# Attention in a hybrid layer on Trainium2: adding DMAs issued apart from their plain loads, and scans a half step later

## The chip, the core and the metric

One core of a Trainium2 chip runs the whole program. The metric is the device time of one execution in microseconds (us), the median over executions. A core has TensorE (PE, matrix products; its weight loads are listed as PEld), VectorE (DVE), ScalarE (ACT), GpSimd (POOL) and SyncE (SP). Each works through its own list of instructions in order and stops at an instruction whose inputs are not there.

## What is computed

One inference step of one decoder layer, for 16 meta tokens, a prompt of 512 tokens and 8 running sequences of 4 new tokens each (560 tokens), width 1024, all in float32:

```python
h = x + 0.5 * rms_norm(swiglu(rms_norm(x, ffn1_pre_g), ffn1_w_gate, ffn1_w_up, ffn1_w_down), ffn1_post_g)
u = rms_norm(h, mix_pre_g)
proj = u @ w_in            # q_a, k_a, v_a, gk_low, r_a of the GLA branch; q_b, k_b, v_b; gate_a, gate_b
...
z = jnp.einsum('bqhd,bkhd->bhqk', qblk, k).astype(jnp.float32) * scale + bias_f
mask = k_idx[None, :] < qi[:, None]
l = jnp.where(mask, jax.nn.log_sigmoid(-z), 0.0)
r = lax.cumsum(l, axis=3, reverse=True) - l
a = jnp.where(mask, jnp.exp(jax.nn.log_sigmoid(z) + r), 0.0)
return jnp.einsum('bhqk,bkhd->bqhd', a.astype(v.dtype), v)
...
m = jax.nn.sigmoid(gate_a) * (o_a @ w_o_gla) + jax.nn.sigmoid(gate_b) * (o_b @ w_o_sb)
h = h + rms_norm(m @ w_out, mix_post_g)
y = h + 0.5 * rms_norm(swiglu(rms_norm(h, ffn2_pre_g), ffn2_w_gate, ffn2_w_up, ffn2_w_down), ffn2_post_g)
```

The change concerns the stick-breaking attention (the middle block): 16 heads of 64, with strictly causal weights. A weight A[t,s] is the sigmoid of its score times the product of (1 - sigmoid) over the later positions before t. The sampled tokens attend to a paged cache as well, in other instructions of the same stages.

## The kernel before

**Stages.** In order of time: FFN1 (to about 400 us), the GLA branch (to about 590), the attention (about 590 to 820), the output products of the mixer, and FFN2. In the attention stage the projections q_b, k_b, v_b are computed for one pair of heads after the other, 8 pairs. Tokens lie on the free axis of a tile, 560 columns in two halves of 280. A float32 product is made of three products of parts in the matmul's own format: hi by hi, hi by lo, lo by hi. So every weight tile that comes from DRAM (a "raw") is first split: ACT casts it to its hi part, and DVE subtracts that from the raw for its lo part (`tt`, L172).

**Order.** The order on PE, DVE, ACT and POOL is the order in which the code emits instructions; only SP's queue, which issues the plain loads, is left to a scheduler. The code counts half steps: one `yield` of a product loop is a half step, some 6 matmuls of 280 columns. `then(n, f)` runs `f` behind half step `n`, `later(d, f)` runs it `d` half steps on. Pair `pr` begins at half step `BEGIN[pr]` = 0, 24, 46, 68, 90, 112, 134, 156. From pair 1 on, its **main** part has 8 half steps of `queries` (`tile_steps`, L723 to L726) and 14 of `values_keys` (`seven_steps`, L1074 hi by hi, L1075 hi by lo, L1076 lo by hi). "Main 3" below is the main part of pair 3, and "+14" is the half step 14 behind its begin.

**The weights of keys and values.** `seven_steps` computes the two products with seven block products in place of eight: it uses b1 twice, t, b2, t, b2, t4, where t and t4 are sums of weight blocks. `weights_at` sets when each of the four is split: hi by `parts_of` (ACT, L1001) and lo by `parted_lo` (DVE, L172). Counted from the pair's begin, b1 has hi at +2 and lo at +3, t has +5 and +6, b2 has +10 and +11, t4 has +13 and +15. PE first uses b2 after +14. Its product goes on into the accumulator d, so the copy e5 of d (ACT, L1054) must have been made by then.

**Adding DMAs.** Two of the sums, t1 and t3, are partly made by the DMA. `Chunks.fetch` takes the next chunk of weights. If it is of kind "adding", it starts plain loads on SP's queue (L644, L645, L652), and issues on POOL's queue a DMA that adds a second operand in place (L648 into the raw, L653 into the room of t3). The adding DMA waits for the plain loads, and it is an instruction in POOL's list. `fetch` runs in main `pr` at +3 (first chunk of pair pr+1), +11 (second chunk) and +18 (the queries' weights of pair pr+2, plain). There are seven DMAs of each of L648 and L653.

**The attention of a pair.** While PE computes main `pr`, the attention of pair `pr`-1 goes on between its half steps, for head 0 and head 1 of the pair (called (0,n) and (1,n), n the part of the score matrix):

- `scores` at +2, +3, +5, +7, +10, +12: PE's products, ACT's two sigmoids (L2002 and L2003: `keep` and `beta`), POOL's masks on `beta` (`affine_select`, L2007).
- `scan` at +3, +3, +5, +6 for head 0 and +8, +9, +11, +13 for head 1: DVE's running product along `keep` (L2016).
- `weigh` at +9 and +14: DVE multiplies `beta` and `keep` (L172, 128x1343), and makes two small copies (L2027). It needs the masks and the scans of its head.
- `turned`, from +15 on: PE transposes the weights (L2078), ACT and DVE make hi and lo of them. The first three calls are for head 0 and the next three for head 1.
- `rows_v` and `rows_k` at +6 and +11 and `tails` at +12: transposes for the new cache rows.

Once, in main 2, `sample_rows` puts a memset and four selects on POOL (L2142 to L2148) at +8, and `sample_rows_out` transposes that on PE (L2160) at +13.

**The end of queries.** The projected queries are scaled and split too: four casts on ACT (L1920) and, for the lo parts, four `stt` on DVE (L175). Behind them four small operations on DVE (L1929) put the sampled tokens' queries into the tiles `qz`.

**Rooms.** Large tiles are taken from and given back to an arena of SBUF; the table `PLACES` says which place each `take` gets. Where a new tile lies on the place of an old one, its writer waits for the old one's readers.

Of the kernel before, what the change touches and what calls it, by code (L numbers as in the profile page):

```python
# [14 lines left out]
ALU = mybir.AluOpType  # L15
# [38 lines left out]
1824062b1f3c5a12107a7792469472788c90324c6a888286487e8e3a68804a0284406c7c643655448a30622f1666607050524e0c3874426e560c  # L54
5e5404340002765957121e5a2e202c2a0c14224a163a68566c7c80643e3c8a3036628444501a4e746e703866422428266001060a3448946a8646
8e924c905a5488325f1a188276727e0d5600025057738c094e5b5d78043e548272075e1c7e0c3c0b835051187f5a8c5976583e1a5306565e5f73
0a4e550c7e8382725a508c3d5276545e065c0b0c58573c83085a733d7e764172555e8c0c5257828d060a583c085476837240590c7e8c578d0655
580c52543c3d823e7606728c598d7e57540f0c0e823c0d76528c7e72949084648e20147c7086600668380e6a086c6224223642803a2c66922e2a
821a4c181c0c4e6a50065a2e540a57092c822a3c6a0b084e2d2f2c820b062b2a4f834e2a2e830b824e2a2c2d2b5a0c422a2e3f3c0b3e82781a83
88386a41541c4a8e6448183c4c7e6c6290348c123050544e32860a6026282441562092701e1563191d4d798f229466842c3e2a2e004b7f89656d  # L60
1b8a49083b096858367459396e72040073027c56403c578a8014686a1658156072569226572825241470719228201e9484223e2c66242e562a14
865c5e628c70063444468e5a4210676c82641876787e88520b4c1c4a3b0f0e482c081a380a66142e257026641258188c305c6c820c9467849224
4a4c767e5e2a627822481c633b3e86205054291e700a66144a082e27644c1a1684948e0e255a5e1f0692672a427e3812783b626386341e227032
76255446524e502324293e6c4482922e7e275658662a42784a18144b708c7a1011060a385e5c3b1c20889008861213302e22921e94846662327e
5a8234425876648e787a388c7027480c5630122a1c1a920d4d11173421821e207e273256182a921248821e5b0c17342c2e7e494d5a2027305692
4821327e34102a82125b561e48190c0e215b181720329227344d827e1c1a102a56481230341e5a2c2e18124d175f327e9256271c1a8216304918
# [70 lines left out]
def hybrid_step(  # L137
# [36 lines left out]
    def stt(out, a, s, b, op0, op1):  # L174
        V.scalar_tensor_tensor(out=out, in0=a, scalar=s, in1=b, op0=op0, op1=op1)  # L175
# [454 lines left out]
    class Chunks:  # L630


        def __init__(self, todo):
            self.todo, self.raws, self.parts, self.early, self.rooms = list(todo), [], [], {}, []
# [2154 lines left out]
```

## Time and profile before

| | |
|---|---|
| executions timed | 1514.03 us median of 3 (1513.37 to 1514.87) |
| the profiled execution | 1517.31 us, of it 1515.6 us span |
| granted TensorE clock, mean | 0.991 |
| PE busy | 1488.7 us, 98% of the span |
| DVE, ACT, POOL busy | 1100.7 (73%), 821.0 (54%), 89.3 (6%) us |
| attention stage, 590 to 820 us | PE busy 211.87 of 230 us |
| adding DMAs, issue to landing, median | 5.2 us (L648), 6.2 us (L653) |

The profile's rows give times in us from the start of the span. In a timeline row stand the start, the duration, the engine, the line and the operation, output and inputs, shapes and, in brackets, how long the engine had been idle before it and what released it. Where rows of one kind follow each other they are one row with a count (x4) and the time from the first one's start to the last one's end. In a table of windows stand, for PE, PEld, DVE, ACT and POOL, the busy time and number of instructions of each, then the granted clock of TensorE (1.00 is full speed), the busy share of the DMA engines and GB/s.

### The profile page before, as it was taken

The page shows a single profiled execution, that of the slowest core. Times are in us where ns is not written, and L with a number is a line of the kernel's source. Part 1 is how long each engine was busy: PE and PEld are TensorE (multiplying, and loading weights), DVE is VectorE, ACT ScalarE, POOL GpSimd, SP SyncE. Part 2 cuts the span into 40 slices and gives each one's busy share as a digit, 9 for nine tenths or more (in the row PEclk, how much of TensorE's full clock was granted, in tenths as well). Part 3 has the DMA queues.
Part 4 walks back from the last instruction along what each step waited for, and adds up shares of the span by engine and source line. Part 5 has one row for each costly group of instructions (what it writes and reads, how often), then busy time and mean ns, then how long its engine had stood idle before and what let it go on. Part 6 is the DMA issues. An engine that isn't in the chain of part 4 may idle for free.

```text
span 1515.6 us, 29815 instructions
## 1 busy us (share of the span) xinstructions
PE 1488.7 (98%) x11825; PEld 1436.4 (95%) x11825; DVE 1100.7 (73%) x1860; ACT 821.0 (54%) x1537; POOL 89.3 (6%) x175
## 2 busy tenths in 40 slices
PE   9999999999999999899999999999999999999998
PEld 8999999999999888788889999999999999999998
DVE  5888888945677767677778745666567998888544
ACT  6445444533655647566777644644565554455434
POOL 2000000000000021321212000000000000000000
PEclk9999999999999999899999999999999999999999
DMA  8133333234664694447566776435532233333343
GB/s 248 54 88 99 98 98 99 86 100 143 165 140 138 161 184 112 100 91 127 122 120 164 213 182 209 101 96 138 158 101 87 87 101 100 108 98 86 89 143 121
DMA packets 288541, 187.61 MB, mean 124 GB/s; under 512 B 10988, under 2 KB 266674, under 8 KB 288402
## 3 DMA queue, kind: packets, MB, share of 16 engines
q1 hardware_dynamic: 280706, 181.97, 45.0%
q0 software_dynamic: 7680, 3.74, 2.4%
q8 instruction: 93, 1.52, 0.4%
q14 instruction: 46, 0.38, 0.1%
q10 hardware_dynamic: 16, 0.00, 0.0%
HBM read 160.63 MB, written 25.03 MB: 123 GB/s over the span
## 4 chain that ended last, share of the span: by engine, by line
PE 91%; DVE 4%; DMA 1%; ACT 1%; issue 1%; POOL 1%; SPq 1%; DVEq 0%; POOLq 0%; ACTq 0%
PE acc L1295 8%; PE acc L1297 8%; PE acc L1296 7%; PE acc L736 6%; PE acc L737 6%; PE acc L739 6%; PE acc L723 5%; PE acc L724 4%; PE acc L726 4%; PE acc L1074 4%; PE acc L1076 4%; PE acc L1075 4%; PE acc L1237 2%; PE acc L1234 2%; PE acc L1235 2%; DVE room L172 1%
## 5 line engine op out<-in xcount | busy, mean ns | idle before, releaser
L172 DVE TENSOR_TENSOR room<-room,room 128x544 f32<-128x544 f32 (+16 forms) x439 | 285.6, 669 | 98.5 <-ACT room L803 18.0
L172 DVE TENSOR_TENSOR lo<-raw,hi 128x1024 fp32r<-128x1024 f32 (+1 forms) x207 | 248.3, 1200 | 82.4 <-ACT hi L701 44.3
L1297 PE MATMUL acc<-room,lo 128*128 128x280 f32 (+1 forms) x896 | 259.6, 290 | 0.0
L1295 PE MATMUL acc<-room,hi 128*128 128x280 f32 (+1 forms) x896 | 259.5, 290 | 0.0
L1296 PE MATMUL acc<-room,hi 128*128 128x280 f32 (+1 forms) x896 | 259.2, 289 | 0.0
L1001 ACT CAST hi<-raw 128x1024 fp32r<-128x1024 f32 x114 | 119.5, 1052 | 141.7 <-PE acc L1296 49.1
L723 PE MATMUL acc<-room,hi 128*128 128x280 f32 x608 | 175.7, 306 | 0.2 <-DVE room L175 0.2
L1295 PEld LDWEIGHTS acc<-room,hi 128*128 128x128 f32 x896 | 168.8, 188 | 0.0
L1296 PEld LDWEIGHTS acc<-room,hi 128*128 128x128 f32 x896 | 168.8, 188 | 0.0
L1297 PEld LDWEIGHTS acc<-room,lo 128*128 128x128 f32 x896 | 168.5, 188 | 0.0
L724 PE MATMUL acc<-room,hi 128*128 128x280 f32 x608 | 163.8, 288 | 0.0
L1074 PE MATMUL acc<-room,hi 128*128 128x280 f32 x476 | 150.1, 315 | 2.2 <-ACT room L1054 1.9
L1076 PE MATMUL acc<-room,lo 128*128 128x280 f32 (+1 forms) x476 | 141.8, 298 | 7.4 <-DVE lo L172 7.4
L1075 PE MATMUL acc<-room,hi 128*128 128x280 f32 (+1 forms) x476 | 140.7, 296 | 0.0
L701 ACT CAST hi<-raw 128x1024 fp32r<-128x1024 f32 (+1 forms) x93 | 93.6, 1006 | 75.8 <-issue 20.4
L1001 ACT CAST hi<-room 128x1024 fp32r<-128x1024 f32 x106 | 88.6, 836 | 81.8 <-PE acc L1296 60.7
L172 DVE TENSOR_TENSOR lo<-room,hi 128x1024 fp32r<-128x1024 f32 x106 | 100.9, 952 | 43.3 <-ACT hi L1001 43.1
L726 PE MATMUL acc<-room,lo 128*128 128x280 f32 x608 | 125.9, 288 | 0.0
L723 PEld LDWEIGHTS acc<-room,hi 128*128 128x128 f32 x608 | 114.5, 188 | 7.3 <-issue 5.6
L724 PEld LDWEIGHTS acc<-room,hi 128*128 128x128 f32 x608 | 114.6, 189 | 0.6
L736 PE MATMUL acc<-room,hi 128*128 128x280 f32 (+2 forms) x388 | 110.7, 295 | 0.0
L737 PE MATMUL acc<-room,hi 128*128 128x280 f32 (+2 forms) x388 | 108.8, 290 | 0.0
(408 smaller groups left out, 3644.1 us busy)
## 6 DMA issues: line engine op xcount, KB each, us to landing
raw<-in_w_in_dram SPq DMA_DIRECT2D x68, 256.0 KB, 4.9
raw<-in_ffn_w_gate_dram SPq DMA_DIRECT2D x64, 256.0 KB, 3.1
raw<-in_ffn_w_up_dram SPq DMA_DIRECT2D x64, 256.0 KB, 3.4
raw<-in_ffn_w_down_dram SPq DMA_DIRECT2D x36, 448.0 KB, 3.8
raw<-in_w_in_dram SPq DMA_DIRECT2D x29, 512.0 KB, 7.9
out_dram<-room SPq DMA_DIRECT2D x36, 256.0 KB, 3.7
room<-in_cache_k_dram SPq DMA_DIRECT2D x32, 256.0 KB, 5.9
room<-in_cache_v_dram SPq DMA_DIRECT2D x32, 256.0 KB, 4.7
```

The costliest lines, as they stand in the source:

```text
L172: (eng or V).tensor_tensor(out=out, in0=a, in1=b, op=op)
L723: T.matmul(acc[h][:, :w], hi[k], act.get(k, h, w)[0], start=(k == order[0]), stop=False, skip_group_check=True)
L724: T.matmul(acc[h][:, : wid[h]], hi[k], a[h][1], start=False, stop=False, skip_group_check=True)
L736: T.matmul(acc[h][:nw, : wid[h]], wh, a[h][0], start=(k == 0), stop=False)
L737: T.matmul(acc[h][:nw, : wid[h]], wh, a[h][1], start=False, stop=False)
L1001: S.copy(hi[:, :kt], src)
L1074: T.matmul(x[:, :n], hi, act_[k][0][:, :n], start=(first and k == 0), stop=False, skip_group_check=True)
L1075: T.matmul(x[:, :w], hi, act_[k][1][:, :w], start=False, stop=False, skip_group_check=True)
L1076: T.matmul(x[:, :w], lo, act_[k][0][:, :w], start=False, stop=(k == 3), skip_group_check=True)
L1295: T.matmul(x[:, :QW], hi, act[k][0], start=(first and k == 0), stop=False, skip_group_check=True)
L1296: T.matmul(x[:, :QW], hi, act[k][1], start=False, stop=False, skip_group_check=True)
L1297: T.matmul(x[:, :QW], lo, act[k][0], start=False, stop=(k == 3), skip_group_check=True)
```

## The change

There are five parts.

1. `fetch` no longer issues the adding DMA; it appends its operands to a list `adds`. A new function `add` issues the next one on POOL's queue. It is called twice in each main 0 to 6, at +14 and +18. The plain loads stay where they were. The main's last mask is emitted at +12.
2. The scans move by a half step: (0,0) and (0,1) from +3 to +4, (0,2) from +5 to +6, (0,3) from +6 to +7, (1,0) from +8 to +9, (1,1) from +9 to +10, (1,2) from +11 to +12, (1,3) from +13 to +14. `weigh` moves from +9 to +10 and from +14 to +15.
3. At +18 the split of the queries' weights becomes `split(1)`, which puts the lo part a half step behind the hi part, and the fetch beside it moves to +20.
4. In `queries` the small `qz` operations now stand between the four casts and the four `stt`.
5. `PLACES` is a new table, so most large tiles lie elsewhere and some waits for rooms differ.

```diff
-            self.todo, self.raws, self.parts, self.early, self.rooms = list(todo), [], [], {}, []
+            self.todo, self.raws, self.parts, self.early, self.rooms, self.adds = list(todo), [], [], {}, [], []
...
                     if r0 == 0:
-                        nc.gpsimd.dma_start(raw[:, 4:], x, accum_op=ALU.add)
+                        self.adds.append((raw[:, 4:], x))
                     else:
                         room = take(KD * P)
                         t3 = room.rearrange("p (k n) -> p k n", n=P)[:, 4:]
                         nc.sync.dma_start(t3, x)
-                        nc.gpsimd.dma_start(t3, w[0][: 4 * P, c0 : c0 + nw].rearrange("(k p) n -> p k n", p=P), accum_op=ALU.add)
+                        self.adds.append((t3, w[0][: 4 * P, c0 : c0 + nw].rearrange("(k p) n -> p k n", p=P)))
...
+        def add(self):
+
+            dst, src = self.adds.pop(0)
+            nc.gpsimd.dma_start(dst, src, accum_op=ALU.add)
...
             self.qs = qs = [take(NP, F32R) for _ in range(2)]
-            for part in range(2):
+            def out(part):
                 for h in range(2):
...
+
+            out(0)
             for e in range(2):
...
                     V.tensor_scalar(out=o, in0=src, scalar1=0.125, scalar2=None, op0=ALU.mult)
+            out(1)
...
-                then(BEGIN[pr] + 18, st.split, 0)
-                then(BEGIN[pr] + 18, st.fetch)
-            pieces = [(2, now.scores, 0, 0), (3, now.scores, 0, 1), (3, now.meta), (3, now.scan, 0, 0), (3, now.scan, 0, 1), (5, now.scores, 0, 2),
-                      (5, now.scan, 0, 2), (6, now.scan, 0, 3), (6, now.rows_v), (7, now.scores, 1, 0), (8, now.scan, 1, 0), (9, now.scan, 1, 1),
-                      (9, now.weigh, 0), (10, now.scores, 1, 1), (11, now.scan, 1, 2), (12, now.scores, 1, 2), (12, now.tails),
-                      (13, now.scan, 1, 3), (14, now.weigh, 1)]
-            pieces.insert(-3, (11, now.rows_k))
+                then(BEGIN[pr] + 18, st.split, 1)
+                then(BEGIN[pr] + 20, st.fetch)
+            if pr < 7:
+                then(BEGIN[pr] + 14, st.add)
+                then(BEGIN[pr] + 18, st.add)
+            pieces = [(2, now.scores, 0, 0), (3, now.scores, 0, 1), (3, now.meta), (4, now.scan, 0, 0), (4, now.scan, 0, 1), (5, now.scores, 0, 2),
+                      (6, now.scan, 0, 2), (7, now.scan, 0, 3), (6, now.rows_v), (7, now.scores, 1, 0), (9, now.scan, 1, 0), (10, now.scan, 1, 1),
+                      (10, now.weigh, 0), (10, now.scores, 1, 1), (12, now.scan, 1, 2), (11, now.rows_k), (12, now.scores, 1, 2), (12, now.tails),
+                      (14, now.scan, 1, 3), (15, now.weigh, 1)]
```

Of `PLACES` the first entries before and after:

```diff
-1824062b1f3c5a12107a7792469472788c90324c6a888286487e8e3a68804a0284406c7c643655448a30622f1666607050524e0c3874426e560c
+06241813202a5c3c5478117282764a7c688e328660846e8c92747a4c7034644e58567e38486a0c04948800401e804290666c8a4452304e500d44
```

The order of instructions, first on POOL in main 1, before. The AFFINE_SELECT rows of L2007 are the masks of pair 0, and the DMA rows are adding DMAs; the brackets name what an instruction waits for (DMAHW and DMASW are transfers that have to land).

```order
L2007 AFFINE_SELECT room_110_5559<-room_110_5559 128x128 [waits Activation_49]
L2007 AFFINE_SELECT room_110_5559<-room_110_5559 128x128
L2007 AFFINE_SELECT room_110_5559<-room_110_5559 128x128 [waits Activation_49]
L648 DMA raw_6752<-in_w_in_dram 128x4x128 [waits DMAHW4_49,DMASW3_49,DMAHW5_49,DMASW2_49,DVE_49]
L2007 AFFINE_SELECT room_110_5559<-room_110_5559 128x128 [waits DMAHW6_49,DMAHW2_49,Activation_49]
L2007 AFFINE_SELECT room_77_4588<-room_77_4588 128x128 [waits DMAHW1_49,Activation_49]
L2007 AFFINE_SELECT room_77_4588<-room_77_4588 128x128
L2007 AFFINE_SELECT room_77_4588<-room_77_4588 128x128 [waits Activation_49]
L653 DMA room_128_6719<-in_w_in_dram 128x4x128 [waits DMASW4_49,DMAHW7_49,DVE_49,PE_49]
L2007 AFFINE_SELECT room_77_4588<-room_77_4588 128x128 [waits DMAHW0_49,Activation_49]
```

The same place after. The masks are now L2015 and the adding DMAs L674.

```order
L2015 AFFINE_SELECT room_76_4272<-room_76_4272 128x128 [waits DMAHW6_49,Activation_49]
L2015 AFFINE_SELECT room_76_4272<-room_76_4272 128x128 [waits DMAHW4_49,DVE_49]
L2015 AFFINE_SELECT room_76_4272<-room_76_4272 128x128 [waits Activation_49]
L2015 AFFINE_SELECT room_76_4272<-room_76_4272 128x128 [waits DMAHW3_49,DMAHW7_49,DMAHW1_49,Activation_49]
L2015 AFFINE_SELECT room_83_4594<-room_83_4594 128x128 [waits PE_49,Activation_49]
L2015 AFFINE_SELECT room_83_4594<-room_83_4594 128x128 [waits PE_49]
L2015 AFFINE_SELECT room_83_4594<-room_83_4594 128x128 [waits PE_49,Activation_49]
L2015 AFFINE_SELECT room_83_4594<-room_83_4594 128x128 [waits Activation_49]
L674 DMA raw_6752<-in_w_in_dram 128x4x128 [waits DMAHW4_49,DMASW3_49,DMAHW5_49,DMASW1_49,DVE_49]
L674 DMA room_77_4273<-in_w_in_dram 128x4x128 [waits DMAHW6_49,DMASW4_49,DVE_49]
```

Before, an adding DMA stands behind the third and behind the seventh mask of main 1. After, all eight masks stand ahead of both adding DMAs.

Then DVE in main 3, from right behind the lo part of t to the lo part of b2, before. The scans are listed as SCALAR_TENSOR_TENSOR of L2016; L175 makes the queries' lo parts, L1929 `qz`, the row of 128x1343 is `weigh` of head 0, and the last row is b2's lo.

```order
L2016 SCALAR_TENSOR_TENSOR room_134_7495<-room_134_7495,room_35_273 128x144 [waits Activation_49]
L175 SCALAR_TENSOR_TENSOR room_133_7374<-acc_7385,room_133_7374 64x280 [waits PE_49,Activation_49]
L175 SCALAR_TENSOR_TENSOR room_133_7374<-acc_7385,room_133_7374 64x280
L175 SCALAR_TENSOR_TENSOR room_133_7374<-acc_7386,room_133_7374 64x232 [waits PE_49,Activation_49]
L175 SCALAR_TENSOR_TENSOR room_133_7374<-acc_7386,room_133_7374 64x232
L1929 TENSOR_SCALAR room_49_871<-acc_7386 64x4x4 x4
L2016 SCALAR_TENSOR_TENSOR room_134_7495<-room_134_7495,room_35_273 128x272
L172 TENSOR_TENSOR room_77_4588<-room_77_4588,room_132_7140 128x1343 [waits DVE_49,Pool_49]
L2027 COPY room_71_4267<-room_77_4588 128x6x16 [waits DVE_49]
L2027 COPY room_71_4267<-room_77_4588 128x6x16
L2016 SCALAR_TENSOR_TENSOR room_134_7495<-room_134_7495,room_35_273 128x400 [waits Activation_49]
L172 TENSOR_TENSOR lo_7554<-raw_7223,hi_7553 128x1024 [waits Activation_49]
```

The same place after, with t's lo as its first row; the scans are L2024, `qz` L1936 and the copies of `weigh` L2035.

```order
L172 TENSOR_TENSOR lo_7471<-room_76_4272,hi_7470 128x1024 [waits DMASW6_49,PE_49,Activation_49]
L2024 SCALAR_TENSOR_TENSOR room_134_7414<-room_134_7414,room_104_5507 128x528
L1936 TENSOR_SCALAR room_84_4595<-acc_7386 64x4x4 [waits PE_49,Activation_49]
L1936 TENSOR_SCALAR room_84_4595<-acc_7386 64x4x4 x3
L175 SCALAR_TENSOR_TENSOR room_133_7374<-acc_7385,room_133_7374 64x280 x2
L175 SCALAR_TENSOR_TENSOR room_133_7374<-acc_7386,room_133_7374 64x232 x2
L2024 SCALAR_TENSOR_TENSOR room_108_5557<-room_108_5557,room_104_5507 128x144
L2024 SCALAR_TENSOR_TENSOR room_108_5557<-room_108_5557,room_104_5507 128x272
L172 TENSOR_TENSOR room_75_4271<-room_75_4271,room_134_7414 128x1343 [waits DVE_49,Pool_49]
L2035 COPY room_78_4307<-room_75_4271 128x6x16 [waits DVE_49]
L2035 COPY room_78_4307<-room_75_4271 128x6x16
L172 TENSOR_TENSOR lo_7553<-raw_7221,hi_7552 128x1024 [waits Activation_49]
```

Head 0's scan of 528 columns, which stood right ahead of t's lo, has come behind it. `qz` has moved ahead of the four L175 and waits for ACT there. The scan of head 1 with 400 columns has left its place ahead of b2's lo; it follows right behind it.

52 lines of the change are left out of this document (26 added, 26 removed).

## The prediction

> **What bounds the kernel now.** I read the page first, then the waits of PE and the windows by stage, then PE's, POOL's, DVE's and ACT's timelines at each wait. PE's busy time on the page:
>
> ```profile
> PE 1488.7 (98%) x11825; PEld 1436.4 (95%) x11825; DVE 1100.7 (73%) x1860; ACT 821.0 (54%) x1537; POOL 89.3 (6%) x175
> ```
>
> The end is PE's, and only PE's idle time and its clock can give anything. In the attention stage, 590 to 820 us, PE has four kinds of waits (columns: us in total, times, longest):
>
> ```profile
> PE acc L1076 <- DVE lo L172: 7.4, 3, 2.9
> PE ps L2078 <- DVE room L172: 5.1, 3, 2.6
> PE ps L2160 <- POOL room L2148: 3.4, 1, 3.4
> PE acc L1074 <- ACT room L1054: 1.9, 3, 0.9
> ```
>
> Together 17.8 us, and no other wait of PE in that stretch. The first and fourth are waits for the weights b2 (lo, and the copy e5); the second is for head 1's weighing; the third is for `sample_rows` in main 2. Three of them on PE, with the wait in brackets; main 1 has the missing 2.3 of the first kind, and main 6 the missing 0.7 of the second:
>
> ```profile
> 611.74 1.12 PE L2078 MATMUL ps<-ident,room 128*128 128x128 f32 x4 [2.63 <-DVE room L172]
> ...
> 673.14 0.60 PE L1076 MATMUL acc<-room,lo 128*128 128x280 f32 x1 [2.27 <-DVE lo L172]
> ...
> 705.39 0.60 PE L1076 MATMUL acc<-room,lo 128*128 128x280 f32 x1 [2.85 <-DVE lo L172]
> ...
> 744.50 0.63 PE L2078 MATMUL ps<-ident,room 128*128 128x128 f32 x4 [1.75 <-DVE room L172]
> ```
>
> A wait costs more than itself, as the granted clock shows (windows; the number behind POOL's is the clock):
>
> ```profile
> 604.90:608.30 3.40, 3.40 (x17) 3.39 (x16) 0.70 (x1) 0.76 (x2) 0.00 (x0) 0.50 0.19 59
> 611.70:615.10 3.40, 3.37 (x15) 3.36 (x16) 2.02 (x5) 1.70 (x3) 0.00 (x0) 0.50 0.58 66
> 639.00:645.90 6.90, 6.90 (x32) 6.87 (x32) 5.33 (x14) 1.32 (x4) 2.06 (x3) 0.51 0.75 139
> 673.20:676.60 3.40, 3.40 (x15) 3.38 (x16) 2.14 (x5) 0.59 (x1) 1.51 (x2) 0.51 0.55 157
> 700.50:703.90 3.40, 1.16 (x7) 0.70 (x6) 2.95 (x5) 3.40 (x8) 2.75 (x5) 0.99 0.99 149
> 703.90:710.70 6.80, 5.31 (x23) 5.29 (x24) 4.72 (x8) 1.41 (x4) 1.60 (x2) 0.50 1.03 191
> 741.40:744.80 3.40, 1.65 (x14) 1.46 (x14) 1.98 (x4) 0.36 (x1) 1.36 (x2) 1.00 0.34 108
> 744.80:748.20 3.40, 3.40 (x30) 3.40 (x29) 2.98 (x5) 3.40 (x8) 0.00 (x0) 1.00 1.14 290
> ```
>
> Behind five waits PE runs at half clock for one or two stretches of 3.4 us: 3.4 + 3.4 + 6.9 + 3.4 + 6.8 = 23.9 us, in which half, 12.0 us, is lost. The window ahead of the fall at 703.9 was idle for 2.24 us; the window 741.4 to 744.8, with 1.75 idle, is followed by full clock. So a window of 3.4 us with about 1.8 us or more idle is followed by half clock. All that could be won here is 17.8 + 12.0 = 29.8 us.
>
> The Trainium skill ("TensorE: Matmul & The Clock Gate", Part 1: The HAM clock gate) says that the clock halves after at least one idle window of about 3.4 us, and warns of gaps longer than that. Here waits of 2.27 and 2.63 us were already followed by half clock, so the trace goes further than the page. By its rule, none of the waits left below would cost clock.
>
> **What holds the masks.** POOL in main 1, and DVE's weighing of head 1 behind it:
>
> ```profile
> 608.49 1.28 POOL L653 DMA_DIRECT2D room<-in_w_in_dram  x1 [7.29 <-PE ps L2078]
> 609.27 0.81 POOL L2007 TENSOR_SCALAR_AFFINE_SELECT room<-room 128x128 f32<-128x128 f32 x1
> ```
> ```profile
> 610.12 1.56 DVE L172 TENSOR_TENSOR room<-room,room 128x1343 f32<-128x1343 f32 x1 [4.52 <-POOL room L2007]
> ```
>
> ```profile
> 600.94 0.71 ACT L2003 ACTIVATE room<-ps,sbb 128x512 f32<-128x512 f32 x1
> ```
>
> POOL stands at the adding DMA L653 (for its plain loads and its room) from 601.2 to 608.49, and only then makes the mask behind it, although ACT's sigmoid for that mask was done at 601.65. DVE waits 4.52 us for that mask, PE 2.63 us for DVE. In main 2 the four selects of `sample_rows` stand behind the other adding DMA (L648), and PE waits 3.40 us for the last of them, L2148.
>
> **The change, part by part.**
>
> *Adding DMAs.* Behind the change both stand behind the main's last mask, so no mask waits for a plain load. In main 1 the last mask can then be made at about 602.5, far ahead of the weighing, and the wait for it goes in whole: 2.63 in main 1, 1.75 in main 5, 0.7 in main 6. In main 2 POOL's masks and selects keep their own time. Ahead of them the DMA's own issue, 1.3 us, goes, so the wait for L2160 shrinks from 3.40 to about 1.9 to 2.1; I take 1.9.
>
> What is moved has to land in time. For the seven DMAs of L653 the trace has:
>
> ```profile
> DMA to landing us min/median/max: 4.6/6.2/14.0
> ```
>
> The first reader of the sum in main 2 is ACT's cast of t:
>
> ```profile
> 627.34 1.05 ACT L1001 CAST hi<-room 128x1024 fp32r<-128x1024 f32 x1
> ```
>
> With 14.0 for the landing and 1.3 for the issue, the DMA has to be issued by 627.3 - 14.0 - 1.3 = 612.0. Before, it was issued at 608.49; now it waits for less on POOL and for another room, and I put it at 606 to 610. Cost: nothing; the cover is the 10 us and more that a landing of the median leaves. The issue on POOL delays nothing, since POOL's next mask belongs to the next main.
>
> *Scans and qz.* These stand in DVE's list, and PE's waits for b2's lo are waits for that list. Here it is in main 3, from t's lo to b2's lo, with two rows of ACT that it waits for:
>
> ```profile
> 659.54 1.30 DVE L172 TENSOR_TENSOR lo<-raw,hi 128x1024 fp32r<-128x1024 f32 x1
> 660.77 0.77 DVE L172 TENSOR_TENSOR room<-raw,room 128x512 f32<-128x512 f32 x1
> 661.47 2.13 DVE L2016 TENSOR_TENSOR_SCAN room<-room,room 128x400 f32<-128x400 f32 x2
> 663.51 1.20 DVE L172 TENSOR_TENSOR lo<-room,hi 128x1024 fp32r<-128x1024 f32 x1
> 664.63 0.45 DVE L2016 TENSOR_TENSOR_SCAN room<-room,room 128x144 f32<-128x144 f32 x1
> 666.08 1.75 DVE L175 SCALAR_TENSOR_TENSOR room<-acc,room 64x280 fp32r<-64x280 f32 x4 [1.00 <-ACT room L1920]
> 667.84 0.53 DVE L1929 TENSOR_SCALAR room<-acc 64x16 f32<-64x16 f32 x4
> 668.40 0.72 DVE L2016 TENSOR_TENSOR_SCAN room<-room,room 128x272 f32<-128x272 f32 x1
> 669.04 1.58 DVE L172 TENSOR_TENSOR room<-room,room 128x1343 f32<-128x1343 f32 x1
> 670.65 0.42 DVE L2027 COPY room<-room 128x96 f32<-128x96 f32 x2
> 670.99 0.98 DVE L2016 TENSOR_TENSOR_SCAN room<-room,room 128x400 f32<-128x400 f32 x1
> 671.89 1.19 DVE L172 TENSOR_TENSOR lo<-raw,hi 128x1024 fp32r<-128x1024 f32 x1
> ```
> ```profile
> 664.75 0.61 ACT L2003 ACTIVATE room<-ps,sbb 128x416 f32<-128x416 f32 x1 [1.04 <-DVE lo L172]
> 665.25 1.54 ACT L1920 ACTIVATE room<-acc 64x280 fp32r<-64x280 f32 x4
> ```
>
> The new order takes one scan, 0.98, from ahead of b2's lo and puts it behind. In exchange `qz` now waits until all four casts L1920 are done, where before the first `stt` began at 666.08, with the casts still running (665.25 to 666.79). Two more scans come behind b1's lo, and the one of 528 columns behind t's. From b1's lo, which has the same inputs and ends at 660.5 (before 660.8), on: two scans 1.0, a sum 0.7 and a scan 0.9 (of the two of 400 and 528 columns) bring DVE to 663.1; t's lo ends at 664.25, where before it ended at 664.7. ACT's sigmoid waited for that, so its four casts end at about 666.4 instead of 666.8. Then qz 0.55, the `stt` 1.75, two scans 1.05, the weighing 1.6, two copies 0.35 and b2's lo 1.2: 666.4 + 6.5 = 672.9. Before it was 673.1, and PE needed it some 2.6 us earlier (2.27 and, just before, a wait of 0.32 for e5). So main 3 keeps 2.6. In mains 1 and 4 the sigmoid of head 1's first scores no longer waits for t's lo, because its room is another one; that is worth up to the 1.04 of the ACT row above. Main 1 stood at 2.27 + 0.75, and I take 2.0; main 4 stood at 2.85 + 0.88 and I take 2.7. In main 2 b2's lo comes 0.4 us after PE is through with `sample_rows`, so 1.9 + 0.4 = 2.3. Mains 5 to 7 had no such wait; by the same list I allow 0.3 in each, 1.0 in all.
>
> The bounds of this term: at best the scan alone counts, 0.98 in each of seven mains, and the waits of the b2 kind come to 9.3 - 4 x 1.0 - 1.0 = 4.3; at worst the 2.13 of the two scans of head 0 is late in each of four mains, and it comes to 9.3 + 8.5. I take the sum above since it follows the list row by row.
>
> *Weighing of head 1.* It is a half step later, behind b2's lo: a scan 0.9, three copies and a sum 0.95, a scan 1.25 and itself 1.6, 4.7 in all. PE, held by the same b2, comes to `turned` of head 1 about 3.9 us after b2 at full clock. So where the clock does not fall, it waits 0.8; where it falls, it waits for nothing.
>
> *Clock.* Four waits of 2.0 to 2.7 remain. With waits of 2.3 at any place of a grid of 3.4, and 1.8 needed in one window, (2.3 + 3.4 - 3.6) / 3.4 = 0.62 of them are followed by half clock. The two long stretches of before followed the longest waits (3.40, 0.88 + 2.85), so I take one stretch each: 4 x 0.62 x 1.7 = 4.2. The other 0.38 x 4 bring the 0.8 of the weighing: 1.2.
>
> *Split and fetch of the queries' weights.* Both are moved by a half step or two, with most of a main, some 30 us, until their use; the lo part then follows a cast that is ready. Nothing. *PLACES*: two new waits of ACT for rooms of about 1.2 us each, and none of PE, in a stretch where PE is not held by ACT: nothing, with 2 us either way in the range.
>
> **The sum.** What remains: 2.0 + 2.3 + 2.6 + 2.7 + 1.0 + 4.2 + 1.2 = 16.0 of 29.8, so 13.8 us go. The profiled execution took 1517.31 us, 3.3 above the median; it would come to 1503.5, and the median from 1514.03 to **1500** us. Own range 1494 to 1506: the sum of the b2 waits with one of four stalls gone or doubled, and the clock falling behind none or all of them.
>
> **Rivals.**
>
> *All waits of PE go, b2's too.* If b2's lo is earlier by more than I work out (by 2.6 in main 3), the clock losses go with it: 29.8 less some 3 of small rests, 1487. For it: a scan of 0.98 does leave. Against it: qz's wait for ACT and the list above. 13%.
>
> *The change does only half of what it says.* The mask waits go, 5.1, with 1.7 of clock behind 611.7 and 1.5 + 1.3 in main 2, but the b2 waits stay in full, and the clock behind them: 9.6 gained, 1504.4. For it: main 3's sum. 12%.
>
> *The clock holds in the gaps that remain.* If only longer idle stretches made it fall, the 4.2 would not be there: 1496. The window from 741.4 speaks for it, the one from 700.5 against. The Trainium skill's page on the clock gate, as cited above, would give this. 5%.
>
> *No gain.* DVE's own list takes the mask's place: head 1's weighing, pushed behind b2's lo, two copies and two scans, is as late in each main as the mask made it in main 1. 2.6 and 1.7 of clock in three or four mains eat 10 to 14 us: 1512 to 1514. Against it: 4.7 us of work against 3.9. 9%.
>
> *Slower.* The second sum lands after ACT's cast of t. ACT then stands in front of the sigmoids and casts, and PE with it. It decides if the adding DMA is issued later than 612.0 and takes 14.0, or much later with the median. At 3 us late in each of seven mains, with 1.7 of clock each, 33 us: 1533. Against it: the median landing of 6.2. 6%.
>
> **How the numbers follow.** My forecast has 55%, the rivals 13, 12, 5, 9 and 6. Three runs lie within 1.5 us of each other, so 0.2%, 3.0 us, is about what can be told: faster is under 1511.0, slower over 1517.1. Faster 0.55 + 0.13 + 0.12 + 0.05 = 0.85; the same 0.09; slower 0.06. The range from 1486 to 1510 holds the first four of these cases and leaves out the last two and a rest of mine.
>
> **What would show it.** In the profile after: no DVE wait on the masks and none of L2160 over 2.5 us; the masks ahead of the DMAs on POOL; b2's waits of PE still 2 to 3 us in mains 1, 3 and 4; three or so half-clock stretches in place of seven. I am wrong if PE's b2 waits are gone (then it is near 1487), if PE waits at `turned` for a weighing that itself waits for nothing (no gain), or if ACT waits for an adding DMA at the cast of t (slower).

## The result, and the profile after

| | before | after |
|---|---|---|
| median of the runs | 1514.03 us (5 runs, 1513.32 to 1516.36) | 1504.86 us (5 runs, 1504.32 to 1506.90) |
| profiled execution, its span | 1517.31, 1515.6 us | 1504.86, 1503.2 us |
| granted clock, mean | 0.991 | 0.997 |

The ratio is 0.9941, with a 95% interval of 0.9927 to 0.9956: 9.2 us faster, where 14.0 were forecast. In the code of after the lines are some 5 to 8 higher; L1076 is now L1081, L1074 L1079, L2078 L2086, L2160 L2168, L2007 L2015, L1054 L1059, L1064 L1069.

PE's busy time on the page, and its four largest waits:

```profile
PE 1484.8 (99%) x11825; PEld 1431.1 (95%) x11825; DVE 1099.9 (73%) x1860; ACT 821.2 (55%) x1537; POOL 78.0 (5%) x175
```
```profile
PE acc L1081 <- DVE lo L172: 3.3, 3, 1.1
PE ps L2086 <- DVE room L172: 2.3, 3, 0.8
PE acc L1079 <- ACT room L1059: 1.8, 3, 1.0
PE ps L2189 <- ACT room L2043: 1.2, 1, 1.2
```

The wait for `sample_rows` (3.4 us) has left the list, the longest wait for head 1's weighing is 0.8 us where it was 2.6, and those for b2's lo are 3 times 1.1 where they were 2.3 to 2.9. L2189 (transposes of cached keys, waiting for a bank that ACT frees) is new. POOL in main 1, from the last two masks on:

```profile
599.96 0.37 POOL L2015 TENSOR_SCALAR_AFFINE_SELECT room<-room 128x128 f32<-128x128 f32 x1 [2.99 <-ACT room L2011]
602.84 0.54 POOL L2015 TENSOR_SCALAR_AFFINE_SELECT room<-room 128x128 f32<-128x128 f32 x1 [2.51 <-ACT room L2011]
603.43 1.28 POOL L674 DMA_DIRECT2D raw<-in_w_in_dram  x1
608.93 1.27 POOL L674 DMA_DIRECT2D room<-in_w_in_dram  x1 [4.22 <-PE ps L2086]
```

A mask now waits for its sigmoid alone. The second DMA still stands 4.22 us, but nothing is behind it. And the clock, at the two places where it still falls (windows that begin and end where the clock changes):

```profile
628.56:631.98 3.42, 2.77 (x21) 2.18 (x19) 3.33 (x7) 2.66 (x5) 0.76 (x2) 1.00 0.00 0
631.98:635.39 3.41, 3.34 (x14) 3.00 (x14) 3.34 (x7) 2.83 (x7) 1.58 (x2) 0.50 0.28 61
662.69:666.11 3.42, 1.67 (x11) 1.44 (x12) 3.35 (x6) 2.89 (x7) 1.56 (x2) 1.00 0.24 70
666.11:669.52 3.41, 3.41 (x17) 3.39 (x17) 3.24 (x6) 1.06 (x2) 1.54 (x2) 0.50 0.77 214
```

Two stretches of 3.4 us at half clock in the attention stage, where there were seven.

**Where the time went.** The same matmul can be looked up in both traces. At 590 us of before, the end of the GLA branch, after is 1.5 us behind; at 850 us of before it is 12.5 us ahead. So the attention gave 14.0 us, FFN1 took 1.5. For each run I take the stretch that was 590 to 850 us before, and add up the gaps between PE's matmuls and the stretches at half clock in it:

| kernel | stretch, us | PE idle, us | at half clock, us |
|---|---|---|---|
| before | 260.0 | 18.1 | 23.9 |
| after | 246.0 | 10.0 | 6.8 |
| adds_alone | 250.0 | 11.5 | 17.1 |
| scans_alone | 255.7 | 19.1 | 13.7 |
| adds_scans | 241.9 | 9.8 | 3.4 |
| adds_back | 258.2 | 20.3 | 13.7 |
| scans_back | 249.4 | 11.6 | 10.2 |
| qz_back | 242.3 | 9.8 | 3.4 |
| split_back | 245.4 | 12.2 | 0.0 |
| places_alone | 256.5 | 19.1 | 13.7 |
| b2_early | 242.6 | 11.6 | 0.0 |
| b2_early_load | 244.5 | 11.7 | 3.4 |
| lighter | 238.6 | 7.7 | 0.0 |

Stretch less idle less 0.45 of the half-clock time is 230 to 232 us in ten of the thirteen rows. So idle time and clock are nearly the whole account. Each row is one execution, not the median: that of before is one of its slower ones (1517.31 us, median 1514.03), that of scans_alone one of its faster (1512.22, median 1514.33).

In after, scans_back and split_back, three of the four kernels with `qz` ahead and the new places (the fourth is adds_back, 231.7), 233 remain: some 2 us that show in PE's list as no wait. Set against qz_back (below), matmul by matmul at full clock, all four have 2.1 to 2.3 us of this kind, and 1.5 to 1.8 of it lies just ahead of L1079 and L2189. A matmul of 280 columns is listed with 0.29 us, while the next starts 0.13 us after it (at 630.09 and 630.22 us of after, for example). So a short wait, or the first part of a longer one, hides under the listed end of the matmul ahead: the L2189 at 723.96 us of after starts 0.30 us further behind the matmul ahead of it than in qz_back, and is listed with 0.14 idle.

### The profile page after: what moved, and what is told of

It reads as the page before. It is cut to its first block, busy times and chain, and to the rows that moved or that the text cites. A ratio compares the mean times of both kernels' runs of the same rounds, so it can differ in the third digit from the quotient of the medians.

```text
span 1503.2 us, 29783 instructions
## 1 busy us (share of the span) xinstructions
PE 1484.8 (99%) x11825; PEld 1431.1 (95%) x11825; DVE 1099.9 (73%) x1860; ACT 821.2 (55%) x1537; POOL 78.0 (5%) x175
## 4 chain that ended last, share of the span: by engine, by line
PE 90%; DVE 5%; ACT 3%; issue 1%; DMA 0%; DVEq 0%; ACTq 0%; SPq 0%
PE acc L1301 8%; PE acc L1302 8%; PE acc L1300 8%; PE acc L741 6%; PE acc L744 6%; PE acc L742 6%; PE acc L728 5%; PE acc L729 4%; PE acc L731 4%; PE acc L1079 3%; PE acc L1081 3%; PE acc L1080 3%; PE acc L1239 2%; PE acc L1242 2%; PE acc L1240 2%; DVE room L172 2%
## 5 line engine op out<-in xcount | busy, mean ns | idle before, releaser
L172 DVE TENSOR_TENSOR room<-room,room 128x544 fp32r<-128x544 f32 (+18 forms) x443 | 286.1, 665 | 83.6 <-ACT room L1059 18.6
L1079 PE MATMUL acc<-room,hi 128*128 128x280 f32 x476 | 147.6, 310 | 2.6 <-ACT room L1059 1.8
L1081 PE MATMUL acc<-room,lo 128*128 128x280 f32 (+1 forms) x476 | 139.9, 294 | 3.4 <-DVE lo L172 3.3
```

The costliest lines, as they stand in the source:

```text
L172: (eng or V).tensor_tensor(out=out, in0=a, in1=b, op=op)
L1079: T.matmul(x[:, :n], hi, act_[k][0][:, :n], start=(first and k == 0), stop=False, skip_group_check=True)
L1081: T.matmul(x[:, :w], lo, act_[k][0][:, :w], start=False, stop=(k == 3), skip_group_check=True)
```

## The experiments

The theory after the result: the masks behind the adding DMAs were one cause, DVE's list ahead of b2's lo and of head 1's weighing the other, and both are paid twice, as waits and as clock. The rivals: that one of the two moves did it all; that the new places of the rooms did it; that `qz` ahead helped. Ratios are to the kernel before, run beside each kernel on the same chip, with 95% intervals.

### One part alone: adds_alone, scans_alone, adds_scans, places_alone

adds_alone is before with `adds`, `add` and the two calls at +14 and +18. 

> The kernel before with the first part of the change alone: the adding DMAs issued at +14 and +18, scans, qz, split and the table of places as before. If the adding DMAs were what held the masks, PE's waits at turned and at sample_rows (5.1 + 3.4 us) go nearly whole, the b2 waits (7.4 + 1.9 us) stay, and with the clock behind the first the time is 1503 to 1507 us. If instead head 1's weighing is late by DVE's own list, so that the scans had to move too, PE waits at turned for a weighing that itself waits for nothing, and the time is 1510 to 1514.

Measured: 1507.14 us, ratio 0.9958 (0.9944 to 0.9972), just above the first case's range. PE's waits in the stage:

```profile
PE acc L1081 <- DVE lo L172: 8.8, 4, 2.2
PE acc L1079 <- ACT room L1059: 2.1, 3, 0.9
```

The waits at `turned` and `sample_rows` are gone to the last, as the first theory said. But PE is then held by b2 in four mains, up to 2.2 us each, with the clock behind all four:

```profile
600.86:604.27 3.41, 1.19 (x9) 1.19 (x10) 3.31 (x8) 1.71 (x5) 1.71 (x2) 1.00 0.48 119
604.27:607.68 3.41, 3.41 (x18) 3.39 (x17) 3.29 (x5) 1.07 (x2) 0.00 (x0) 0.50 0.56 107
631.58:634.99 3.41, 1.30 (x9) 1.07 (x9) 3.35 (x7) 2.69 (x7) 1.62 (x2) 1.00 0.52 121
634.99:638.40 3.41, 3.41 (x17) 3.39 (x17) 3.31 (x9) 0.59 (x1) 1.34 (x2) 0.50 0.94 139
```

scans_alone is before with the other scans and weighings:

```diff
-            pieces = [(2, now.scores, 0, 0), (3, now.scores, 0, 1), (3, now.meta), (3, now.scan, 0, 0), (3, now.scan, 0, 1), (5, now.scores, 0, 2),
+            pieces = [(2, now.scores, 0, 0), (3, now.scores, 0, 1), (3, now.meta), (4, now.scan, 0, 0), (4, now.scan, 0, 1), (5, now.scores, 0, 2),
...
```

> The kernel before with the scans and weighings a half step or so later and nothing else. If the two moves add up, the scans bring alone what they bring on top of the moved DMAs, 8.4 us, and the time is 1504 to 1507 us. If they need each other, because the masks stay late behind the DMAs and the weighings are later still, the time is 1512 to 1518.

Measured: 1514.33 us, ratio 1.0001 (0.9992 to 1.0010): nothing. POOL and DVE in main 1 show why:

```profile
608.13 1.28 POOL L653 DMA_DIRECT2D room<-in_w_in_dram  x1 [9.02 <-DMA room<-in_w_in_dram]
608.92 0.81 POOL L2007 TENSOR_SCALAR_AFFINE_SELECT room<-room 128x128 f32<-128x128 f32 x1
```
```profile
609.77 1.56 DVE L172 TENSOR_TENSOR room<-room,room 128x1343 f32<-128x1343 f32 x1 [4.51 <-POOL room L2007]
```

The mask comes when the DMA's inputs are there, at 608.9, whatever happens ahead of it. What b2 gave back (9.3 to 6.5 us), PE waits longer at `turned`: 10.5 us, 5.1 of it in main 1.

adds_scans is adds_alone with these scans too, on the places of before. 

> The kernel before with the adding DMAs and the scans and weighings moved, and nothing else: its own table of places, qz behind the lo parts of the queries, split as before. If the new places cost the early load's collision in FFN1 (1.1 us at 375 us) and the 1.2 us of an ACT wait for a room, and qz ahead cost 3 to 4 us, this one takes 1498 to 1501. If the new places were needed so that ACT's sigmoids don't wait for t's lo, the b2 waits stay above 6 us and it takes 1502 to 1505.

Measured: 1498.71 us, ratio 0.9901 (0.9887 to 0.9916): the first case's time. (L2083 here is L2086 of after.)

```profile
PE acc L1081 <- DVE lo L172: 6.2, 4, 1.7
PE ps L2083 <- DVE room L172: 2.8, 3, 1.2
PE acc L1079 <- ACT room L1059: 0.9, 2, 0.5
```

So the later scans need the moved DMAs: 6 us and 0 alone, 15 together. Against adds_alone PE idles only 1.7 us less; the rest is clock, 3.4 us at half in place of 17.1. The waits of 2.2 us became waits of 1.2 to 1.7, at b2 and later at `turned`. The waits for b2's lo stay above 6 us, which was the second case's sign, but with the new places they do too (6.1 us in qz_back below); the new places take away only the 0.9 us for e5.

places_alone is before with the table of places of after. 

> The kernel before with the table of places of the changed kernel and nothing else. If the new places only cost (1.1 us for the early load in FFN1, 1.2 us for ACT's wait for a room), the time is 1514 to 1517 us. If they free ACT's sigmoids from t's lo and so shorten the b2 waits, 1509 to 1513.

Measured: 1516.37 us, ratio 1.0015 (1.0007 to 1.0024). The new places cost some 2 us, and nearly all of it lies in FFN1. In each of the eight kernels with the new places PE falls 0.7 us behind before between 50 and 350 us, spread over many matmuls (each under 0.06 us in this run; why was not looked for), and, except in b2_early_load, 1.0 to 2.0 us more at 375 us; the kernels with the old places do neither. These are PE's wait at 375 us in after, and on SP's queue the early load of 512 KB for the GLA values, in before and in after:

```profile
376.24 0.40 PE L744 MATMUL acc<-room,lo 128*128 128x280 f32 x1 [0.73 <-DVE lo L172]
```
```profile
374.18 0.58 SPq L674 DMA_DIRECT2D room<-in_w_in_dram  x1
```
```profile
364.27 0.43 SPq L679 DMA_DIRECT2D room<-in_w_in_dram  x1
```

In the new table that load's room is free 10 us earlier, so it is issued earlier, among the loads of FFN1's weights. One of those lands late, and PE loses 1.1 us. This is tested in b2_early_load below.

In the attention the waits of places_alone mostly trade places. The largest is in main 4, where b2's lo holds PE for 5.84 us (before: 2.85): POOL stands at an adding DMA, and head 0's weighing, which DVE has ahead of b2's lo, waits for the masks behind it.

```profile
698.71 1.28 POOL L648 DMA_DIRECT2D raw<-in_w_in_dram  x1 [9.25 <-DMA raw<-in_w_in_dram]
```
```profile
700.34 1.64 DVE L172 TENSOR_TENSOR room<-room,room 128x1343 f32<-128x1343 f32 x1 [3.71 <-POOL room L2007]
```

So a mask behind an adding DMA can hold b2's lo as well as `turned`; in after DVE waits for no mask.

### One part taken back: adds_back, scans_back, qz_back, split_back

Each is after with one part as before. adds_back:

```diff
-                        self.adds.append((raw[:, 4:], x))
+                        nc.gpsimd.dma_start(raw[:, 4:], x, accum_op=ALU.add)
...
-                then(BEGIN[pr] + 14, st.add)
-                then(BEGIN[pr] + 18, st.add)
```

> The changed kernel with the adding DMAs issued at the fetch again, all else as changed. If they are the cause of the mask waits, these come back on PE at turned and at sample_rows (5.1 + 3.4 us before), with the clock behind them, and the time is 1510 to 1515 us. If the later scans and weighings alone give the masks the time that they need, the waits stay under 3 us and the time is 1505 to 1508.

Measured: 1517.97 us, ratio 1.0028 (1.0017 to 1.0038): slower than before, and above the ranges of both cases.

```profile
PE ps L2086 <- DVE room L172: 8.6, 4, 4.8
PE acc L1081 <- DVE lo L172: 7.4, 4, 4.1
```

The waits at `turned` are back, 4.8 us of them in main 1. The one at `sample_rows`, which the first case expected too, is not. Instead PE waits 4.1 us for b2's lo in main 4, in the way of places_alone: POOL stands 9.29 us at the adding DMA, DVE 2.67 us at the masks behind it. The second theory, that later scans and weighings give the masks time, is out.

scans_back has the list of `pieces` of before. 

> The changed kernel with scans and weighings back at the half steps of before. If the later scans are what made the b2 waits smaller (from 9.3 us to 5.1), these come back to about 8 us, the three waits at turned (2.3 us) go, and the time is 1506 to 1510 us. If the scans' place doesn't matter (the b2 waits shrank by the new places of the rooms), it stays at 1503 to 1506.

Measured: 1507.84 us, ratio 0.9958 (0.9945 to 0.9972), 3.0 us slower than after by the medians, 2.6 by the ratios, whose intervals overlap (after: 0.9927 to 0.9956). So the waits have to carry the reading:

```profile
PE acc L1081 <- DVE lo L172: 6.2, 4, 1.6
PE acc L1079 <- ACT room L1059: 1.7, 3, 1.0
PE acc L1079 <- ACT acc L1069: 1.3, 2, 0.9
```

That is 9.2 us around b2, where after has 3.3 + 1.8 + 0.5, and none is at `turned`. The first theory holds.

qz_back:

```diff
             out(0)
+            out(1)
             for e in range(2):
...
                     V.tensor_scalar(out=o, in0=src, scalar1=0.125, scalar2=None, op0=ALU.mult)
-            out(1)
```

> The changed kernel with the qz operations back behind the four lo parts of the queries. If qz's wait for all four casts of ACT costs DVE time, the lo of b2 comes 0.5 to 0.9 us earlier, the b2 waits fall from 5.1 to 2 or 3 us, and the time is 1501 to 1504. If the order is worth something (ACT's casts and the banks of the accumulators come free earlier), the time is 1506 to 1508. If neither, 1504 to 1506.

Measured: 1501.31 us, ratio 0.9918 (0.9904 to 0.9931), 3.5 us faster than after (1500.99 to 1502.45 us against 1504.32 to 1506.90). The time is as the first case said, its mechanism only in part. From the end of t's lo to the end of b2's lo DVE takes 7.76 us in main 3 in place of 8.50, so b2's lo is 0.7 us earlier, as that case said; but the b2 waits don't fall to 2 or 3 us. What else goes is a wait on ACT: main 3 in after, and in qz_back:

```profile
656.95 1.54 ACT L1925 ACTIVATE room<-acc 64x280 fp32r<-64x280 f32 x4
660.06 0.38 ACT L1069 COPY acc<-acc 128x280 f32<-128x280 f32 x1 [1.57 <-DVE room L175]
```
```profile
655.87 1.55 ACT L1925 ACTIVATE room<-acc 64x280 fp32r<-64x280 f32 x4
657.70 0.38 ACT L1069 COPY acc<-acc 128x280 f32<-128x280 f32 x1 [0.28 <-DVE room L175]
```

ACT's L1069 copies one accumulator into the bank that the queries had, and has to wait until DVE's `stt` have read it. With `qz` ahead the `stt` begin only behind all four casts and four more operations, and ACT's whole list behind L1069 is 1.3 us later: e5, the frees of banks for L2189, the next sigmoids. The waits for e5 (1.8 us) and half of L2189's are gone in qz_back; those for b2's lo are longer (6.1 us), since PE is there earlier. Some 2 of the 3.5 us are hidden waits as described above, most of them at L1079 and L2189.

split_back has `st.split, 0` and the fetch at +18. 

> The changed kernel with the split of the queries' weights as before: lo right behind hi at +18, the fetch at +18. If nothing waits there, as I forecast, 1504 to 1506 us. If the lo part, waiting 1.2 us for its cast on DVE ahead of the keys' sums, was a cost in seven mains that the change took away, 1507 to 1511.

Measured: 1504.33 us, ratio 0.9939 (0.9925 to 0.9953), as after. Nothing waits there.

### What is left: b2_early, b2_early_load, lighter

b2_early goes on from qz_back. The fetch that used to hang on b2's lo is put at +11 by a line of its own (the line that takes it off b2's lo is not shown):

```diff
-                weights_at(then, BEGIN[pr] + TILE, ("kv", pr), (-6, -6, -5, -4), t=(-3, -2), b2=(2, 3), t4=(5, 7))
+                weights_at(then, BEGIN[pr] + TILE, ("kv", pr), (-6, -6, -5, -4), t=(-3, -2), b2=(1, 2), t4=(5, 7))
+                then(BEGIN[pr] + 11, st.fetch)
...
-                      (10, now.weigh, 0), (10, now.scores, 1, 1), (12, now.scan, 1, 2), (11, now.rows_k), (12, now.scores, 1, 2), (12, now.tails),
+                      (10, now.scores, 1, 1), (11 if pr < 7 else 10, now.weigh, 0), (12, now.scan, 1, 2), (11, now.rows_k), (12, now.scores, 1, 2), (12, now.tails),
```

> The changed kernel with qz back behind the lo parts of the queries, and b2's split a half step earlier (hi at +9, lo at +10), head 0's weighing at +11 behind it. If DVE's list ahead of b2's lo is what PE waits for, the b2 waits fall from 6.1 us to under 1.5 and the time from 1501.3 to 1494 to 1498. If head 0's weighing, 1.9 us later, then holds turned of head 0 as long, the wait only changes its name and the time is 1500 to 1503.

Measured: 1501.35 us, ratio 0.9918 (0.9904 to 0.9933), as qz_back.

```profile
PE ps L2086 <- DVE room L172: 9.2, 7, 1.9
```

No wait for b2 is left, and the one at `turned` has grown from 2.8 to 9.2 us. Most of it, 6.8 us, is at head 1, not at head 0 as the second case said. The wait changed its name: what binds is the sum of DVE's work between the queries and the weighings, not its order.

b2_early_load is b2_early with the early load issued by ACT, 16 half steps later:

```diff
-            nc.sync.dma_start(room.rearrange("p (k n) -> p k n", n=2 * P),
-                              win[r0 : r0 + 4 * P, c0 : c0 + 2 * P].rearrange("(k p) n -> p k n", p=P))
+            later(16, lambda: nc.scalar.dma_start(room.rearrange("p (k n) -> p k n", n=2 * P),
+                                                win[r0 : r0 + 4 * P, c0 : c0 + 2 * P].rearrange("(k p) n -> p k n", p=P)))
```

> The kernel with b2's split earlier, and in FFN1 the early load of the GLA values' weights issued by ACT some 10 us later (at about 374 us, as in the kernel before, where its room came free then). If this load's collision with FFN1's loads is what cost 1.1 us at 375 us, that goes, and the time is 0.7 to 1.5 us under the kernel without this edit. If the delay had another cause, the two are within 0.3 us.

Measured: 1501.70 us, ratio 0.9917 (0.9903 to 0.9931); between the medians no gain shows. In its trace PE's wait of 0.7 us in FFN1 is gone: between the matmuls at 370 and 375 us of before, b2_early falls back by 1.2 us and this kernel by nothing, as the theory says. But the profiled execution has one stretch at half clock in the attention where b2_early has none. The cause in FFN1 is shown in the trace; the forecast gain in time is not, and that the clock of the runs hides it is likely but not shown.

lighter is adds_scans with three small jobs off DVE:

```diff
-                V.tensor_copy(am[:, i : i + 2, :, e], src.unsqueeze(2).to_broadcast([P, 2, 3, NM]))
+                G.tensor_copy(am[:, i : i + 2, :, e], src.unsqueeze(2).to_broadcast([P, 2, 3, NM]))
...
-            V.tensor_copy(tk[:NTL], p[:NTL, :P])
+            S.copy(tk[:NTL], p[:NTL, :P])
...
-            V.tensor_copy(tail_v[pr // 4][:NTL, fc], p[:NTL, P : 2 * P])
+            S.copy(tail_v[pr // 4][:NTL, fc], p[:NTL, P : 2 * P])
```

> The kernel before with DMAs and scans moved, and three small jobs taken off DVE's list: the two copies of each weighing on POOL (0.33 us a weighing) and two of the copies of the tails on ACT (0.5 us). If DVE's list between the queries and head 1's weighing is what PE waits for (6.2 us for b2's lo, 2.8 us at turned), each b2 wait falls by 0.3 us and those at turned nearly vanish: 1495 to 1497 us. If POOL's copies run against DVE's, or ACT's delay the copies that PE needs, 1498 to 1500.

Measured: 1496.85 us (4 runs, 1495.33 to 1500.04), ratio 0.9891 (0.9876 to 0.9905).

```profile
PE acc L1081 <- DVE lo L172: 4.5, 4, 1.2
PE ps L2083 <- DVE room L172: 2.0, 5, 0.8
```

Each b2 wait fell by 0.4 us, and the clock doesn't fall once in the stage. The waits at `turned` shrank less than expected. It is the lowest of all, 17 us under before; its interval and that of adds_scans overlap, so the step between the two is shown by the waits and not by the time.

## Why the prediction was right, and where not

The direction and the range held (1504.86 in 1486 to 1510, and within the forecast's own 1494 to 1506). By its steps:

- **The adding DMAs: right, one size off.** No mask waits for a load, ACT waits for no adding DMA at the cast of t, and the second was issued at 608.93 (put at 606 to 610). For `sample_rows` I took 1.9 us to stay; 0.14 us at most stayed. I had taken off the DMA's issue alone and left POOL's own work at its durations, and the four selects took 1.6 us where before they took 4.0 (why, is below). Its last select of `sample_rows`, before and after:

```profile
637.19 1.14 POOL L2148 TENSOR_SCALAR_AFFINE_SELECT room<-room 32x64 f32<-32x64 f32 x1
```
```profile
628.57 0.39 POOL L2156 TENSOR_SCALAR_AFFINE_SELECT room<-room 32x64 f32<-32x64 f32 x1
```

  The cover for the landing was much thinner than the 10 us that I had worked out. The moved DMAs landed later, 10.8 us behind the issue in the median (before: 5.2 and 6.2): that of 608.93 landed at 619.5, and ACT cast t at 622.34. One sum on DVE, at 617.13, did wait 1.3 us for the landing, and PE not at all. So the rival *slower* came nearer than I had thought.

- **b2's lo: the list was right, the wait not.** In main 3 it ended at 663.70 + 1.22 = 664.92. PE is 8.14 us ahead of before at that place, so this is 673.06 on the clock of before, where I had worked out 672.9 and before had 673.1. I gave the mains 2.0, 2.3, 2.6 and 2.7; they took 1.5, 0.5, 2.1 and 1.5. (In main 3 I also forgot to take off the 0.2 that I had just worked out, 673.1 - 672.9.) The 1.0 for mains 5 to 7 did not come. In main 3 the wait comes in two parts:

```profile
663.34 0.40 PE L1079 MATMUL acc<-room,hi 128*128 128x280 f32 x1 [1.03 <-ACT room L1059]
...
664.97 0.40 PE L1081 MATMUL acc<-room,lo 128*128 128x280 f32 x1 [1.10 <-DVE lo L172]
```

- **`qz`: its cost was looked for in the wrong list.** I priced its wait for ACT on DVE alone, where it was about right. It falls as well on ACT's copies behind L1069, and through them on e5 and on the banks of L2189. By qz_back both together cost 3.5 us.
- **Head 1's weighing: right in size, three times in place of 1.5.** I worked out 0.8 us each; the three waits at `turned` are 0.7 to 0.8.
- **The clock behind the waits that stay:** 4.2 us forecast, two stretches, 3.4 us. In part this is luck: one of the two, at 631.98, came behind a window with 0.65 us idle, where by my rule none was due.
- **PLACES: "nothing, with 2 us either way" was wrong.** It cost about 2 us by places_alone, nearly all of it in FFN1, where I had not looked. And I had taken the b2 waits of mains 1 and 4 to shrink by the new places, by 2.0 us together; between adds_scans and qz_back, the nearest pair, only the 0.9 us for e5 goes (6.2 and 6.1 us for b2's lo). The PE wait of 1.2 at L2189 behind ACT's L2043, which I had called hidden, is not the places' alone: it is 0.2 in places_alone, none in adds_scans and 0.6 in qz_back.
- **The sum:** I left 16.0 of 29.8 us. The profile after has 9.4 of waits and 3.4 of clock, 12.8. By that sum 17 us should have gone, but the stage gave 14.0. Of the difference, 0.9 is that half clock costs 0.45 and not 0.5 of its time ((23.9 - 6.8) x 0.05), and some 2 are the waits hidden under matmuls, which come with `qz`.
- **From the profile to the median.** I took the whole gain of one profiled execution off the median. But the profiled execution of before was one with much half clock. Of 13 runs of before beside adds_alone, the five with a mean clock of 0.991 or 0.992 took 1514.3 to 1517.7 us, the eight with 0.993 to 0.996 took 1512.9 to 1513.8. Beside the other kernels (36 runs) the tendency is the same but the two groups overlap: 1514.5 to 1516.3 and 1511.6 to 1516.8. So the clock is part of it. Between the two profiled executions the gain is 1517.31 - 1504.86 = 12.5 us, near the 13.8; between the medians it is 9.2, since the median run of before had less to lose.
- **By the medians alone** the miss of 4.8 us reads in another way. The two moves gave 14.8 us (adds_scans), one more than the 13.8 that I worked out for the whole change. Then `qz` took back 3.5 (qz_back) and the places 2.5 (places_alone), which I had at nothing or nearly: 14.8 - 3.5 - 2.5 = 8.8, and 9.2 came. So it is partly luck that the time came within 5 us of the forecast: I gave the two moves too little and the other parts no cost.

Of the rivals, *half of what it says* gave 1504.4, near what came, but by another way: it kept the b2 waits at 9.3 us, and they came to 5.1. The mechanism of *no gain*, a weighing made late by DVE's own list, is real but small, 0.7 to 0.8 us three times; its price was also added up wrongly, since 2.6 + 1.7 in three or four mains is 13 to 17 us and not 10 to 14. In scans_alone and adds_back the weighing is late for another reason, a mask behind a DMA. *The clock holds* is out: it fell behind a window with 1.75 us idle (662.69 to 666.11). With that, the rule of the Trainium skill ("TensorE: Matmul & The Clock Gate", Part 1), by which only idle windows of about 3.4 us count, would have given no half clock here, and there were two stretches.

## What to carry to other kernels

An instruction that waits for a transfer belongs behind the compute of its queue that others need, and its neighbours' times have to be moved with it: here one move alone gave 6 us, the other none, and both 15. It still has to land in time: here one landed 2.8 us ahead of its reader. When an engine's list is the limit, another order only renames the wait (b2_early); taking work off the list shortens it (lighter). Before you carry a gain from one profiled execution to the median, look at how much of that execution's time was a matter of chance, here in part the clock. And price the small parts of a change too: two that looked free took back 6 of 15 us here.

## What the runs showed of the hardware

How long PE must idle for its clock to fall has no sharp edge here. In scans_alone two windows with the same 1.82 us idle went apart:

```profile
696.21:699.63 3.42, 1.60 (x11) 1.15 (x9) 3.11 (x6) 3.42 (x8) 3.14 (x5) 1.00 0.82 128
699.63:703.04 3.41, 2.43 (x11) 2.42 (x12) 3.31 (x7) 0.56 (x2) 0.00 (x0) 0.50 1.08 214
737.17:740.59 3.42, 1.60 (x14) 1.41 (x13) 2.31 (x4) 0.69 (x2) 1.04 (x2) 1.00 0.38 120
740.59:744.00 3.41, 3.41 (x30) 3.41 (x30) 2.95 (x7) 3.27 (x8) 0.00 (x0) 1.00 1.13 277
```

In the attention every stretch at half clock lasts 3.41 us or twice that, so I cut each trace into windows of 3.41 us that these stretches fit. Over the windows of all thirteen traces, those at full clock with 1.63 to 1.86 us of idle time were followed by either; none with 1.88 or more was followed by full clock. Three windows with less were followed by half clock: 0.65 us idle in after (628.56 to 631.98), 0.98 in adds_back and 1.09 in scans_back. All three hold the nine small matmuls of `sample_rows_out` (in adds_back all but the first one), a transpose of 32x32 and eight of one column. If these are counted as idle, the three windows have 1.66, 1.90 and 2.11 us. In the seven kernels where the clock did not fall behind these matmuls, their windows have 1.43 or less by the same count. So all thirteen traces agree with such small matmuls counting as idle time; no run tried it by itself.

The time of one of POOL's selects depends on what runs beside it. The 64 masks of 128x128 in before and in after, as a group (busy, then mean ns of one):

```profile
L2007 POOL TENSOR_SCALAR_AFFINE_SELECT room<-room 128x128 f32<-128x128 f32 x64 | 42.9, 878 | 137.4 <-ACT room L2003 137.4
```
```profile
L2015 POOL TENSOR_SCALAR_AFFINE_SELECT room<-room 128x128 f32<-128x128 f32 x64 | 27.7, 441 | 194.9 <-ACT room L2011 190.4 <-issue 3.1 <-PE ps L2007 1.4
```

The adding DMAs alone don't explain it: the mean is 878 ns in before, 875 in places_alone, 711 in scans_alone and 651 in adds_back, where the DMAs stand among the masks, but scans_back, where they stand behind, has 736; the other kernels with the DMAs behind have 370 (lighter) to 585. What DVE does meanwhile explains more. Over the thirteen traces, 232 masks ran with no DVE instruction beside them and no adding DMA being issued, and every one took 282 to 297 ns. Those that began while an adding DMA was still being issued took 878 in the mean (69 masks). Of the others, those beside a product or difference of two tiles on DVE (TENSOR_TENSOR) took 752 in the mean and up to 2.6 us (379), those beside a scan 602 (113). The selects of `sample_rows` fit: the two long ones of before, 1.55 and 1.14 us, ran beside DVE's weighing and a scan, and none of the four in after did. This is read off the traces and no run tried it apart, and spans on POOL are rough.
